# Attention mixed with the query and half of the output projections in one written TensorE order, with the residual parked in DRAM

## The chip, the cores and the metric

The kernel runs on one core of a Trainium2 chip. The metric is device time in microseconds (us), from the first to the last instruction of the program with what lies around it, as the median over runs.

## What is computed

One inference step of a two-layer decoder: layer 0 is a Mamba-2 mixer with a SwiGLU feed-forward, layer 1 is a sliding-window attention with a SwiGLU feed-forward. There are 1,104 rows of width 1,024: 1,024 prompt rows, 16 learned meta rows and 64 sampled rows (8 sequences of 8). The change lies between the two feed-forwards. Cut to that part, the reference is:

```python
kv_in = _rmsnorm(h, p['kv_norm_g'])                      # h: residual after layer 0
k_new = _rope_partial((kv_in @ p['w_k'])..., pos)        # 4 heads of 64
v_new = (kv_in @ p['w_v'])...
q = _rope_partial((_rmsnorm(h, g) @ p['w_q'][i])..., pos)  # 16 heads of 64
s = einsum(q, k) * HEAD_DIM**-0.5                        # masked to the last 128 keys
m = maximum(max(s), sink)
p = exp(s - m); p = p / (sum(p) + exp(sink - m))
h = h + einsum(p, v) @ p['w_o'][i]                       # output projection and residual
hn = _rmsnorm(h, p['ffn_norm_g'][layer])                 # and the second feed-forward on it
```

All arithmetic is fp32. Large products are done as three fp32r matmuls on a high and a low part of each operand (`mm3`, L71 to L73); attention uses plain fp32 matmuls.

## The kernel before, in words

**Order of work.** The program is written with a tile framework whose planner puts the instructions of each engine in order, by their place in the program and by simulated readiness; `tc.high_priority(n)` moves a block forward in that choice. `in_order` (L1001) chains a list of instructions of one engine, so that the planner keeps their written order. `mix(a, b, na, nb)` (L1020) advances two generators in the ratio na to nb while the program is written. All loads and stores that concern us are issued by one queue, SP's, in order.

**Stages around the change.** They follow each other on TensorE:

1. The layer-0 feed-forward ends with its down projection (`FeedForward.down`). Its input factors `bo` come from DRAM, six buffers. For each finished tile of 128 features, `Prepare.tile` squares it and splits it into operands for the next stage. The residual stays in SBUF as `K.h[0]` and `K.h[1]` (two column halves of 552: 40 sampled or meta columns and 512 prompt columns).
2. `qkv`: nine row blocks are multiplied by the key and value weights, then by the query weights in two halves of 512 columns (`rows_mm`, 24 matmuls of 512 columns for each block and half; `few_rows_mm` for the sampled rows). A finished block is scaled by ScalarE, rotated on GpSimd (`rope_rows`, six operations) and turned by four TensorE transposes into `A.QT` (`turn_queries`, L1963).
3. Attention: 16 units (`PromptUnit`: eight blocks of 128 queries, two head groups `a`), each with `scores(0)`, `scores(1)` (L2018, TensorE; L2024, masked maximum on VectorE), `softmax` (L2042, eight exponentials on ScalarE; L2045, two products on GpSimd), `turn` (12 transposes, L2060; copies L2063 and L2067) and `values` (L2078, L2082). Beside them `attend_sample` works through the eight sampled sequences in four steps each: keys turned (L2116), scores (L2127, L2128), a softmax on VectorE, ScalarE and GpSimd (L2140), its transposes (L2143, L2144), values (L2154, L2155). The planner is free to order all this on TensorE.
4. Output projection: attention's results are split into high and low parts (`split_copy`, L77 and L78), and for each column half e of 544 and each of eight feature tiles m, `output_tile` makes 48 matmuls of 272 columns, adds the product to the residual in place (L2179), squares the sum (L2180) and stores it to `F.saved` for the end of the second feed-forward. Its weights `wo` come through `F.units`, whose pool is opened after `qkv`.
5. `scale_early` and `early` prepare half 0 for the second feed-forward during the tiles of half 1 (`scaled`, L1272).

Of the kernel before, what the change touches and what calls it, by code (L numbers as in the profile page):

```python
# [51 lines left out]
ANA = 30  # L52
ANB = 33
# [1141 lines left out]
class FeedForward:  # L1195
# [50 lines left out]
    def save(self, e, m=None):  # L1246
# [7 lines left out]
        if self.layer == 0:  # L1254
            if e == 0:
                to(0, 0, h[0][:, :, 40:592])
                to(1, 0, h[0][:, :, 0:40])
            else:
                to(1, 40, h[1])
        elif m is not None:  # L1260
            to(e, 32, h[e][:, :, 40:552])
        elif e == 0:
            to(0, 0, h[0][:, :, 0:24])
            to(0, 24, h[1][:, :, 32:40])
        else:
            to(1, 0, h[1][:, :, 0:32])
# [7 lines left out]
    def few(self, dst, srcs, c):  # L1274
# [3 lines left out]
        o = 0  # L1278
        for s in srcs:
            w = s.shape[2]  # L1280
            rb = K.tot[:, c + o : c + o + w].unsqueeze(1).broadcast_to([128, KD, w])
            nc.vector.tensor_tensor(t[:, :, o : o + w], s, rb, ALU.mult)
            o += w
        nc.vector.tensor_tensor(dst, t, self.gain.unsqueeze(2).broadcast_to([128, KD, n]), ALU.mult)

    def scale_early(self, pool, psS):
# [12 lines left out]
        if self.layer:  # L1299
            self.few(h0[:, :, 8:40], [h0[:, :, 0:24], K.h[1][:, :, 32:40]], 0)  # L1300
# [41 lines left out]
    def late(self, k):  # L1342
# [3 lines left out]
        if self.layer and k == 0:  # L1346
            self.few(K.h[1][:, :, 8:40], [K.h[1][:, :, 0:32]], self.h)
# [418 lines left out]
class RowWeights:  # L1766
# [5 lines left out]
    def get(self, src, gain, stage, depth=KD):  # L1772
        nc, out = self.nc, []

        def load(k):
            if k < KD:
                t = stage(k)
                for a, b, s in src:
                    nc.sync.dma_start(t[:, a:b], s[128 * k : 128 * k + 128, :])
                out.append(t)  # L1780

        for k in range(depth):
            load(k)
        for k in range(KD):
            H = self.pool.tile([128, 512], F32R, name="rwH", tag="rwH", bufs=KD)
            L = self.pool.tile([128, 512], F32R, name="rwL", tag="rwL", bufs=KD)
            g = gain[:, k : k + 1]
            nc.scalar.activation(H[:], out[k], AF.Copy, scale=g)
            nc.vector.scalar_tensor_tensor(L[:], out[k], g, H[:].bitcast(F32), ALU.mult, ALU.subtract)
            out[k] = (H, L)  # L1790
            load(k + depth)
        return out


class Prepare:
# [5 lines left out]
    def __init__(self, tc, K, I):  # L1801
# [3 lines left out]
        self.U = [[None] * KD, [None] * KD]  # L1805

# [5 lines left out]
    def step(self, c, p):  # L1812
        I, K = self.I, self.K
        if c == 1 and p == 1:
            self.few = [self.wp.tile([128, KD, NX], F32R, name="ux" + x, tag="ux" + x) for x in "HL"]
            self.kv = self.weights.get([(0, 256, I["w_k"]), (256, 512, I["w_v"])], K.g_kv, lambda k: K.tot[:, 512 * (k % 2) : 512 * (k % 2) + 512], 2)
# [9 lines left out]
    def tile(self, e, m):  # L1826
# [20 lines left out]
        split_copy(nc, H, L, src)  # L1847
        self.seen[e] += 1
        if self.seen[e] == KD:
            self.small(e)  # L1850

# [25 lines left out]

def qkv(tc, K, A, ap, psS, I, O, pre):

    nc = tc.nc  # L1880
    with ExitStack() as st:
        en = lambda **kw: st.enter_context(tc.tile_pool(reuse_waits="tile", **kw))
        st.callback(pre.stack.close)
        fp = en(name="qf", bufs=1)
        psP = en(name="qps", bufs=4, space=PSUM)
        w = pre.kv
        cs = lambda i, n: A.rope[:n, 8 * i : 8 * i + 8]
        sn = lambda i, n: A.rope[:n, 72 + 8 * i : 80 + 8 * i]
        size = lambda i: 128 if i else NX
        start = lambda i: NX + 128 * (i - 1) if i else 0  # L1890
        r, r8 = {}, {}

        def scales(which, nm):
            blocks = [(128 * (i - 1) if i else 1024, size(i)) for i in which]
            t = row_scale(K, blocks, ap, psS.tile([128, 512], F32, name="ps", tag="s"))
            t8 = ap.tile([128, len(which)], F32, name=nm)
            nc.vector.tensor_scalar(t8[:], t[:], HD ** -0.5, None, ALU.mult)
            for x, i in enumerate(which):
                r[i], r8[i] = t[:, x : x + 1], t8[:, x : x + 1]

        def rows_mm(i, w):
            n = size(i)
            ps = psP.tile([128, 512], F32, name="rps", tag="rps")
            for k in range(KD):
                mm3(nc, ps[:n, :], *pre.operand(k, i), w[k][0][:], w[k][1][:], k == 0, k == KD - 1)
            return ps

        def few_rows_mm(w):

            ps = psP.tile([128, 512], F32, name="rps", tag="rps")  # L1910
            for k in range(KD // 2):
                for q in range(2):
                    f = KD // 2 * q + k
                    nc.tensor.matmul(
                        ps[64 * q : 64 * q + 64, :], hs[:, f, :], w(f), start=k == 0, stop=k == KD // 2 - 1, tile_position=(0, 64 * q)
                    )
            t = K.tot[:NS, 512:1024]
            nc.scalar.copy(t, ps[64:, :])
            nc.vector.tensor_tensor(t, t, ps[:64, :], ALU.add)
            return t  # L1920

        def put_kv(i, ps):
            n, o = size(i), start(i)
            kr = fp.tile([128, 256], F32, name="kr", tag="kr", bufs=2)
            nc.scalar.mul(kr[:n], ps[:n, 0:256], r[i][:n])
            nc.scalar.mul(A.V[:n, i, :], ps[:n, 256:512], r[i][:n])
            rope_rows(nc, fp, kr[:n], n, NKV, cs(i, n), sn(i, n), nc.gpsimd)
            pt = psS.tile([128, 512], F32, name="ps", tag="s")
            for a in range(2):
                nc.tensor.transpose(pt[:, 128 * a : 128 * a + n], kr[:n, 128 * a : 128 * a + 128], K.ident[:n, :n])  # L1930
            nc.scalar.copy(A.KT[:, :, o : o + n], pt[:, :256].rearrange("p (a c) -> p a c", a=2)[:, :, :n])
            if i == 0:
                pt = psS.tile([128, 512], F32, name="ps", tag="s")
                for kv in range(NKV):
                    nc.tensor.transpose(pt[:64, 64 * kv : 64 * kv + 64], kr[:NS, 64 * kv : 64 * kv + 64], K.ident[:NS, :NS])
                nc.scalar.copy(A.KS[:].rearrange("p a b -> p (a b)"), pt[:64, :256])
                for nm, t in (("k_s", kr[:NS]), ("v_s", A.V[:NS, 0, :])):
                    nc.sync.dma_start(O[nm][:, 120:128].rearrange("b l h d -> b l (h d)"), t)
            if i == 8:
# [441 lines left out]
```

## Time and profile before

| what | us |
|---|---|
| median of 3 runs | 2922.55 |
| lowest and highest run | 2916.72, 2922.65 |
| the profiled execution, its own time | 2921.38 |
| its span, first to last instruction | 2919.6 |
| TensorE busy by the page | 2804.8 |
| mean granted TensorE clock | 0.975 |

The profile is of one execution. "PE" is TensorE's matmuls, "PEld" its weight loads, "DVE" VectorE, "ACT" ScalarE, "POOL" GpSimd, "SP" the queue that issues transfers. Matmuls are pipelined: the time that one is said to last overlaps the next, so what it costs is read as the distance from its start to the next start. The granted clock is 1.00 at TensorE's full level (2.4 GHz) and 0.50 at the lower one (1.2 GHz).

### The profile page before, as it was taken

Reading aid. Unit: us, or ns where it says so; the run is one execution under the profiler, and the core shown is the slowest. Engines: PE = TensorE matmul, PEld = TensorE weight load, DVE = VectorE, ACT = ScalarE, POOL = GpSimd, SP = SyncE. Lnnn points to the kernel's source line nnn. Section 1 sums busy time; section 2 is a strip of 40 time slices with the busy share of each in tenths; the row PEclk is TensorE's granted clock in tenths of the full one; section 3 lists DMA queues with packets and bytes.
Section 4 is the critical chain, followed back from the end, with each engine's and each line's share of the span. In section 5 each row is a group of like instructions: output and inputs, shape, how many; then the busy total and the mean of one; then the engine's idle time right before and its main releaser. Section 6 shows DMA issues by size and latency. Waiting matters only on the chain.

```text
span 2919.6 us, 51250 instructions
## 1 busy us (share of the span) xinstructions
PE 2804.8 (96%) x19990; PEld 2577.6 (88%) x19990; DVE 2024.0 (69%) x3669; ACT 1218.7 (42%) x2592; POOL 494.9 (17%) x694
## 2 busy tenths in 40 slices
PE   7989999999999999999999999999998999999998
PEld 7878988887787799999999997765898999999998
DVE  6778676647574698777778771265469878777787
ACT  4666554346442344333332242256434433433224
POOL 1455444215122100000000002333120000000000
PEclk9999999999999999999999999969999999999999
DMA  6776866565454424444377640021232534437664
GB/s 205 238 232 190 282 200 208 188 234 202 169 181 149 159 97 168 135 146 149 135 282 281 221 146 33 22 65 36 68 89 78 178 129 157 150 136 293 239 226 154
DMA packets 321377, 485.44 MB, mean 166 GB/s; under 512 B 23967, under 2 KB 222047, under 8 KB 320081
## 3 DMA queue, kind: packets, MB, share of 16 engines
q1 hardware_dynamic: 321134, 482.15, 48.7%
q8 instruction: 158, 2.59, 0.4%
q14 instruction: 85, 0.70, 0.1%
HBM read 311.24 MB, written 170.84 MB: 165 GB/s over the span
## 4 chain that ended last, share of the span: by engine, by line
PE 68%; DVE 5%; ACT 2%; DMA 1%; issue 1%; POOL 0%; SPq 0%; ACTq 0%; DVEq 0%
PE wacc L1476 10%; PE wacc L1474 10%; PE wacc L1475 10%; PE dacc L1474 5%; PE dacc L1475 5%; PE dacc L1476 5%; PE acc L71 2%; PE acc L72 2%; PE acc L73 2%; PE rps L71 2%; PE rps L72 2%; PE rps L73 2%; PE po L2078 1%; PE ps L2018 1%; PE wacc L71 1%; PE wacc L72 1%
## 5 line engine op out<-in xcount | busy, mean ns | idle before, releaser
L1134 ACT CAST wo<-ws 128x512 fp32r<-128x512 f32 x428 | 263.7, 620 | 567.7 <-PE wacc L1475 222.9
L1474 PE MATMUL dacc<-bo,wo 128*128 128x276 f32 (+1 forms) x1232 | 359.3, 292 | 11.9 <-DMA bo<-f_B 7.8
L1475 PE MATMUL dacc<-bo,wo 128*128 128x276 f32 (+1 forms) x1232 | 356.7, 290 | 0.0
L1476 PE MATMUL dacc<-bo,wo 128*128 128x276 f32 (+1 forms) x1232 | 356.6, 290 | 0.0
L1135 DVE TENSOR_TENSOR wo<-ws,wo 128x512 fp32r<-128x512 f32 x428 | 300.3, 706 | 48.9 <-ACT wo L1134 30.1
L71 PE MATMUL acc<-uH,wH 128*128 128x296 f32 (+1 forms) x840 | 279.5, 333 | 1.9 <-DVE th L760 1.6
L72 PE MATMUL acc<-uL,wH 128*128 128x296 f32 (+1 forms) x840 | 278.0, 331 | 0.0
L73 PE MATMUL acc<-uH,wL 128*128 128x296 f32 (+1 forms) x840 | 276.4, 329 | 0.9 <-DVE wL L154 0.9
L1474 PEld LDWEIGHTS dacc<-bo,wo 128*128 128x128 f32 x1232 | 233.1, 189 | 13.8 <-issue 11.8
L1475 PEld LDWEIGHTS dacc<-bo,wo 128*128 128x128 f32 x1232 | 233.0, 189 | 0.0
L1476 PEld LDWEIGHTS dacc<-bo,wo 128*128 128x128 f32 x1232 | 232.9, 189 | 0.0
L71 PEld LDWEIGHTS acc<-uH,wH 128*128 128x128 f32 x840 | 161.4, 192 | 17.1 <-issue 5.0
L72 PEld LDWEIGHTS acc<-uL,wH 128*128 128x128 f32 x840 | 161.3, 192 | 12.0 <-issue 3.4
L73 PEld LDWEIGHTS acc<-uH,wL 128*128 128x128 f32 x840 | 160.9, 192 | 11.6 <-issue 2.0
L583 DVE SCALAR_TENSOR_TENSOR cc<-raw,convw,cc 128x616 f32<-128x616 f32 (+1 forms) x144 | 136.0, 947 | 40.6 <-ACT cc L581 38.6
L1622 DVE TENSOR_TENSOR hN<-hN,dacc 128x544 f32<-128x544 f32 (+1 forms) x164 | 116.4, 721 | 30.4 <-PE dacc L1476 25.5
L71 PE MATMUL acc<-yH,wH 128*128 128x296 f32 (+1 forms) x360 | 122.7, 341 | 8.8 <-ACT yH L77 5.2
L1058 POOL MEMSET rv<- 128x5 f32 (+1 forms) x6 | 0.6, 104 | 729.8 <-PE dacc L1476 723.5
L72 PE MATMUL acc<-yL,wH 128*128 128x296 f32 (+1 forms) x360 | 120.4, 335 | 0.0
L73 PE MATMUL acc<-yH,wL 128*128 128x296 f32 (+1 forms) x360 | 120.2, 335 | 0.0
L1474 PE MATMUL wacc<-N4H,wo 128*128 128x276 f32 (+1 forms) x352 | 102.0, 290 | 4.4 <-DVE hN L1487 2.4
L1474 PE MATMUL wacc<-T2H,wo 128*128 128x276 f32 (+1 forms) x352 | 101.8, 291 | 4.2 <-ACT T2H L77 4.2
(575 smaller groups left out, 8519.3 us busy)
## 6 DMA issues: line engine op xcount, KB each, us to landing
kept<-wH SPq DMA_DIRECT2D x56, 512.0 KB
kept<-wL SPq DMA_DIRECT2D x56, 512.0 KB
ws<-ffn_w_gate SPq DMA_DIRECT2D x44, 512.0 KB
ws<-ffn_w_up SPq DMA_DIRECT2D x44, 512.0 KB
ws<-ffn_w_down SPq DMA_DIRECT2D x44, 512.0 KB
ws<-ssm_w_in SPq DMA_DIRECT2D x40, 512.0 KB
wH<-kept SPq DMA_DIRECT2D x38, 512.0 KB
wL<-kept SPq DMA_DIRECT2D x38, 512.0 KB
```

The source lines that it names most:

```text
L71: nc.tensor.matmul(out, wH, xH, start=start, stop=False)
L72: nc.tensor.matmul(out, wH, xL, start=False, stop=False)
L73: nc.tensor.matmul(out, wL, xH, start=False, stop=stop)
L583: nc.vector.scalar_tensor_tensor(o, raw[:, k : k + n], w(k), o, ALU.mult, ALU.add)
L1134: nc.scalar.copy(H, src)
L1135: (low or nc.vector).tensor_tensor(L, src, H.bitcast(F32), ALU.subtract)
L1474: nc.tensor.matmul(out, wH, xH, start=start, stop=False, skip_group_check=True)
L1475: nc.tensor.matmul(out, wH, xL, start=False, stop=False, skip_group_check=True)
L1476: nc.tensor.matmul(out, wL, xH, start=False, stop=stop, skip_group_check=True)
L1622: add = lambda d, s: nc.vector.tensor_tensor(d, d, s, ALU.add)
L2018: nc.tensor.matmul(ps[e][:, 192 * s : 192 * s + kn], QT[es, hp, s], A.KT[es, a, self.k0[s] : self.k0[s] + kn], start=True, stop=True)
L2078: nc.tensor.matmul(out[s][e], A.V[:n, i + s, vs[e]], self.PT[e][:n, 256 * s : 256 * s + 256], start=True, stop=False)
```

## The change

The query projection, attention and half 0 of the output projection no longer follow each other; they are written interleaved, and TensorE keeps the written order from the first query block to the end of half 0.

- The units go through all blocks of head group 0 first, then of group 1. After three query blocks (`LEAD`), the other 13 are written between the steps of units 0 to 13 and of the sampled sequences, by `mix(att, qs, 96, 104)`: a query step is one of eight parts of a block (three matmuls), an attention step is one of `scores`, `turn` of one e, `values`, or a step of a sampled sequence.
- After the query weights are released, the weight pool opens, the results of twelve units and of the sampled rows are split with high priority, five attention steps go ahead (`AHEAD`), and the rest of attention is mixed with half 0 of the output projection (`output_early`), 4 to 5; a step there is two of the eight parts of a 272-column accumulation.
- PSUM: four rings of two banks (scores, turned, out, rows) take the place of three scores, three turned, two out and, in `qkv`, four rows.
- Attention's work tiles lie where the residual was (`A.space` on the tags h0 and h1). So the residual is stored to `F.saved` as the layer-0 feed-forward ends (`keep`, 16 tiles and three small pieces), `output_early` loads, adds to and stores one tile at a time, and both halves are loaded again before `output_tile`, which now does half 1 alone, with its TensorE instructions in written order. The stores of the finished half 0 take the place of those that were there before.

```diff
-def mix(a, b, na=1, nb=1):
+def joined(a, b, na=1, nb=1):      # as mix was, with a yield after each step
+def mix(*args):
+    for _ in joined(*args):
+        pass
...
+    def keep(self, e, fs):         # called by Prepare.tile and after its last tile
+        h, put = self.K.h[e], lambda i, a, b, o, n: self.nc.sync.dma_start(self.saved[i][:, fs, a:b], h[:, fs, o : o + n])
+        if fs.stop - fs.start == 1:
+            put(e, 32, 544, 40, 512)
...
+    w_q = lambda a: [(0, 512, I["w_q"][0][:, 512 * a : 512 * a + 512])]
+    raw = [[pre.weights.load(w_q(a), k, A.QT[:, k, a]) for k in range(KD)] for a in range(2)]
...
+    with tc.high_priority(PRIO):
+        w = [pre.weights.split(k, raw[0][k], K.g_attn) for k in range(KD)]
+    put_kv(*late.pop(0))
+    A.space = [K.cp.tile([128, n], F32, name="work", tag=f"h{e}") for e, n in enumerate((4736, 4416))]
...
+    def queries(w):
+        turned = [sampled_turned]
+        for a in range(2):
+            for i in range(1, 9):
+                for k, acc in enumerate(rows_mm(i, w)):
+                    if k == 5 and turned:
+                        turned.pop(0)()
+                    if k == KD - 1:
+                        dst = fp.tile([128, 512], F32, name="qr", tag="row", bufs=2)[:]
+                        put_q(i, acc, dst)
+                        turned.append(lambda i=i, a=a, dst=dst: turn_queries(i, a, dst))
+                    yield
...
+def output_early(nc, K, F, sqh, rows, oH, oL):
+    for m in range(KD):
+        u = F.units.get(1)
+        w = [u.factor(nm) for nm in ("lo", "hi")]
+        x = F.units.raw()[:, :544]
+        nc.sync.dma_start(x, F.saved[0][:, m])
+        F.units.load(2)
+        for c in range(2):
+            acc = rows()
+            cs = slice(272 * c, 272 * c + 272)
+            for k in range(KD):
+                wH, wL = (t[:, 128 * (k % 4) : 128 * (k % 4) + 128] for t in w[k // 4])
+                mm3(nc, acc[:, :272], wH, wL, oH[:, k, cs], oL[:, k, cs], k == 0, k == KD - 1)
+                if k == KD - 1:
+                    nc.vector.tensor_tensor(x[:, cs], x[:, cs], acc[:, :272], ALU.add)
+                    output_square(nc, K, F, sqh, x[:, cs], 0, m, 272 * c)
+                    if c:
+                        nc.sync.dma_start(F.saved[0][:, m], x)
+                if k % 2:
+                    yield
...
+                def prompt(first, last, done=lambda u: None):
+                    n = len(units)
+                    for x in range(first, last):
+                        if x < n:
+                            units[x].scores(0)
+                            yield
+                        if x >= 2:
+                            units[x - 2].turn(0)
+                            yield
+                        if x < n:
+                            units[x].scores(1)
+                            yield
+                        if 0 <= x - 1 < n:
+                            units[x - 1].softmax()
+                        if x >= 2:
+                            units[x - 2].turn(1)
+                            yield
+                            units[x - 2].values()
+                            done(units[x - 2])
+                            yield
+                forced = len(traced)
+                for _ in range(8 * LEAD):
+                    next(qs)
+                sample = attend_sample(tc, K, A, sp, ps, I, O, (4, 5, 6, 7, 0, 1, 2, 3))
+                att = joined(prompt(0, EARLY), sample, 5 * EARLY - 6, 32)
+                mix(att, qs, 5 * EARLY - 6 + 32, 8 * (16 - LEAD))
+            pre.stack.close()
             F.open_weights("left")
...
+            with tc.high_priority(PRIO):
+                for e, o, a, b in ((0, 0, 40, 64), (0, 24, 32, 40), (1, 0, 0, 32)):
+                    split_copy(nc, OH[e][:, :, o : o + b - a], OL[e][:, :, o : o + b - a], A.OS[:, :, a:b])
+                for u in units[: EARLY - 2]:
+                    split(u)
+            early = output_early(nc, K, F, sqh, ps.rows, OH[0], OL[0])
+            att = prompt(EARLY, len(units) + 2, split)
+            for _ in range(AHEAD):
+                next(att)
+            mix(att, early, 4, 5)
+            in_order(tc, traced[forced:], nc.tensor)
+            K.h = [K.cp.tile([128, KD, 552], F32, name=f"hN{e}", tag=f"h{e}") for e in range(2)]
+            for e in (1, 0):
+                for m in range(0, KD, 2):
+                    nc.sync.dma_start(K.h[e][:, m : m + 2, 8:552], F.saved[e][:, m : m + 2])
```

Here LEAD is 3, EARLY 14 and AHEAD 5. In the diff, comments behind a # are added for the reader.

## Rows read from the trace of the kernel before

**Rows 1.** The page, busy time over the whole span.
```profile
PE 2804.8 (96%) x19990; PEld 2577.6 (88%) x19990; DVE 2024.0 (69%) x3669; ACT 1218.7 (42%) x2592; POOL 494.9 (17%) x694
```

**Rows 2.** Windows: end of down projection, queries, attention, output half 0, half 1.
```profile
core 0: us, PE busy (x) PEld busy (x) DVE busy (x) ACT busy (x) POOL busy (x), PEclk, DMA share, GB/s
1562.00:1733.00 171.00, 170.65 (x1343) 170.43 (x1341) 142.59 (x225) 49.42 (x82) 0.14 (x2) 1.00 0.58 201
1787.70:1892.30 104.60, 104.60 (x477) 80.15 (x477) 18.50 (x27) 23.18 (x50) 33.30 (x113) 1.00 0.06 18
1892.30:2063.70 171.40, 158.34 (x1033) 101.18 (x1031) 97.80 (x466) 93.68 (x382) 56.82 (x62) 0.82 0.15 44
2063.70:2116.30 52.60, 49.01 (x385) 48.41 (x386) 26.76 (x49) 21.70 (x48) 7.79 (x5) 1.00 0.31 93
2116.30:2176.40 60.10, 56.20 (x431) 55.11 (x430) 39.58 (x79) 21.63 (x47) 17.91 (x8) 0.97 0.35 102
```

**Rows 3.** Windows: attention at the lower clock, and the rest of it.
```profile
1897.60:1945.40 47.80, 45.62 (x196) 27.97 (x198) 25.55 (x122) 22.59 (x94) 13.12 (x14) 0.50 0.30 83
1945.40:2063.70 118.30, 108.81 (x804) 70.39 (x800) 69.09 (x338) 69.74 (x285) 41.26 (x38) 0.94 0.10 30
```

**Rows 4.** Timeline of TensorE in attention: start, duration, line, operation, count, [idle before].
```profile
1957.24 0.92 PE L2018 MATMUL ps<-KT,QT 64*128 64x192 f32 x8
1958.09 0.66 PE L2060 MATMUL pq<-cmask_sb,P 128*128 128x128 f32 x4
1958.67 1.08 PE L2078 MATMUL po<-PT,V 128*64 128x256 f32 x4
1959.68 0.66 PE L2082 MATMUL po<-PM,V 64*64 64x256 f32 x8
1960.28 0.66 PE L2060 MATMUL pq<-cmask_sb,P 128*128 128x128 f32 x4
...
1965.33 1.56 PE L2018 MATMUL ps<-KT,QT 64*128 64x192 f32 x12
1966.83 0.30 PE L2154 MATMUL pq<-PTd,vst 128*64 128x32 f32 x2
1967.06 0.62 PE L2116 MATMUL pq<-cmask_sb,kst 128*64 128x128 f32 x4
1967.61 0.30 PE L2155 MATMUL pq<-PTd,V 64*64 64x32 f32 x2
...
1969.22 1.53 PE L2060 MATMUL pq<-cmask_sb,P 128*128 128x128 f32 x12
1970.68 0.44 PE L2127 MATMUL ps<-kT,q 64*32 64x128 f32 x8
...
1971.17 0.92 PE L2018 MATMUL ps<-KT,QT 64*128 64x192 f32 x8
...
1978.27 0.33 PE L2143 MATMUL pq<-cmask_sb,PD 128*128 128x128 f32 x1 [0.85 <-POOL PD L2140]
```

**Rows 5.** Timeline of TensorE in the query projection.
```profile
1803.36 0.39 PE L71 MATMUL rps<-rwH,u 128*128 128x512 f32 x1
...
1804.06 0.40 PE L71 MATMUL rps<-rwH,u 128*128 128x512 f32 x1
```

**Rows 6.** Groups by line in attention: ScalarE, VectorE, GpSimd (busy, mean ns, idle before).
```profile
L2042 ACT ACTIVATE P<-P,nm 128x192 f32<-128x192 f32 x112 | 49.5, 445 | 7.3 <-DVE es L2035 7.3
L2063 ACT COPY PT<-pq 128x512 f32<-128x512 f32 x28 | 15.9, 580 | 15.1 <-PE pq L2060 15.1
L2045 POOL TENSOR_TENSOR P<-P,sm 128x768 f32<-128x768 f32 x28 | 41.0, 1466 | 53.0 <-DVE sm L2044 39.7 <-DVE es L2035 7.7 <-DVE sm L2043 3.0
```

**Rows 7.** Groups by line in output half 0, VectorE.
```profile
L78 DVE TENSOR_TENSOR OL<-O,OH 128x544 fp32r<-128x544 f32 x16 | 10.5, 720 | 0.9 <-ACT OH L77 0.6
```

**Rows 8.** The chain that ended last, around half 1 of the output projection.
```profile
2139.67 3.60 DVE hN L1272 x6
```

More of the change, by code (lines that the diff above doesn't have):

```diff
@@ L51 @@
 FIRST = 3
-ANA = 30
-ANB = 33
+LEAD = 3
+EARLY = 14
+AHEAD = 5
+PLACES = {"scores": ("S", 2), "turned": ("T", 2), "out": ("O", 2), "rows": ("P", 2)}
 HALVES = (
@@ L1770, in __init__, with load, split @@
         self.nc, self.pool = nc, pool
[L1772 to L1792, printed above, removed]
+    def load(self, src, k, t):
+        for a, b, s in src:
+            self.nc.sync.dma_start(t[:, a:b], s[128 * k : 128 * k + 128, :])
+        return t
+    def split(self, k, t, gain):
+        nc = self.nc
+        H = self.pool.tile([128, 512], F32R, name="rwH", tag="rwH", bufs=KD)
+        L = self.pool.tile([128, 512], F32R, name="rwL", tag="rwL", bufs=KD)
+        g = gain[:, k : k + 1]
+        nc.scalar.activation(H[:], t, AF.Copy, scale=g)
+        nc.vector.scalar_tensor_tensor(L[:], t, g, H[:].bitcast(F32), ALU.mult, ALU.subtract)
+        return H, L
 class Prepare:
@@ L1875, in close, with qkv @@
         pass
[L1878 removed]
+def qkv(tc, K, A, ap, fp, ps, O, I, pre):
     nc = tc.nc
[L1881 to L1939, printed above, removed]
[L1940 to L1987 removed]
@@ new lines, in rows_mm, with few_rows_mm @@
+    def rows_mm(i, w):
+        n = size(i)
+        acc = ps.rows()
+        for k in range(KD):
+            mm3(nc, acc[:n, :], *pre.operand(k, i), w[k][0][:], w[k][1][:], k == 0, k == KD - 1)
+            yield acc
+    def few_rows_mm(w):
+        acc = ps.rows()
+        for k in range(KD // 2):
+            for q in range(2):
+                f = KD // 2 * q + k
+                nc.tensor.matmul(
+                    acc[64 * q : 64 * q + 64, :], hs[:, f, :], w[f], start=k == 0, stop=k == KD // 2 - 1, tile_position=(0, 64 * q)
+                )
+        t = K.tot[:NS, 512:1024]
+        nc.scalar.copy(t, acc[64:, :])
+        nc.vector.tensor_tensor(t, t, acc[:64, :], ALU.add)
+        return t
@@ new lines, in qkv, with __init__, ring, get @@
+    return queries(w)
+class Space:
+    def __init__(self, work):
+        self.work, self.used, self.rings = work, [0, 0], {}
+    def ring(self, name, where, size, count):
+        o = self.used[where]
+        self.used[where] += size * count
+        assert self.used[where] <= self.work[where].shape[1]
+        self.rings[name] = [[self.work[where][:, o + size * i : o + size * i + size] for i in range(count)], 0]
+    def get(self, name, rows=128):
+        r = self.rings[name]
+        r[1] += 1
+        return r[0][(r[1] - 1) % len(r[0])][:rows]
@@ L2236, in attention @@
             F.units.queue += ups
[L2237 removed]
+            F.units.load(2)
             so = ExitStack()
             op = so.enter_context(tp(name="ao", bufs=1))
[L2240 to L2242 removed]
@@ new lines, in attention @@
+        steps, tiles = iter(()), []
+        for m in range(KD):
+            at = len(traced)
+            with tc.high_priority(60 if m else 0):
+                output_tile(nc, K, F, sqh, OH[1], OL[1], m)
+            tiles += traced[at:]
+            for _ in range(3):
+                next(steps, END)
+            if m == 0:
+                steps = chain(F.scale_early(F.wp, F.psS), F.early())
+        in_order(tc, tiles, nc.tensor)
+        for _ in steps:
+            pass
+        with tc.high_priority(PRIO):
+            F.late_scale(F.psS)
```

415 lines of the change are left out of this document (203 added, 212 removed).

## The prediction

> **What bounds the kernel now.** I read the page first. It puts TensorE at 96% of the span [rows 1], and a reader could stop there: at most 4% would be left. So the second view is the windows by stage. In the query projection TensorE is busy throughout at the full clock, with its weight loads at 80.15 of 104.6 us. In attention the two rows part: matmuls are busy 158.34 of 171.4 us, weight loads only 101.18, and the mean clock is 0.82 [rows 2]. The third view cuts attention at its clock. For 47.8 us the clock is at its lower level, and in the other 118.3 us it has dips (0.94) [rows 3]. No other engine is full: VectorE 97.80, ScalarE 93.68, GpSimd 56.82 of 171.4 us [rows 2]. So attention has neither a full TensorE nor a full neighbour: it waits in chains between engines.
>
> How much TensorE attention really needs I take from the timeline at the full clock, by distances between starts, because durations overlap. Eight score matmuls take 0.85 us (1957.24 to 1958.09) and twelve 1.50 (1965.33 to 1966.83), so 0.1175 each; sixteen transposes 0.58 + 1.46, so 0.1275 each; four L2078 take 1.01, eight L2082 0.60 [rows 4]. A unit has 16, 12, 8 and 8 of them: 1.88 + 1.53 + 2.02 + 0.60 = 6.03 us, and 16 units 96.5. A sampled sequence has four key transposes (0.55), scores (1970.68 to 1971.17, 0.49), two transposes (0.26) and 16 small value matmuls at 0.23 a pair, as the last seven pairs show (1967.61 to 1969.22), 1.84: 3.14 us, eight of them 25.1. The last turned queries and the sampled queries (8 and 16 transposes, the latter smaller, at up to 0.1275) add some 2 us. The stage needs 123.6 us and takes 171.4: **47.8 us are surplus**. Half of the slow stretch, 23.9 us, is the clock; the other half is waiting that busy time hides.
>
> The Trainium skill (Perfetto Trace Analysis, Identifying the Most-Contended Engine) says that matmul busy time is a poor measure of TensorE's headroom and names weight-load busy time as a good one. The trace agrees: 92% by matmuls, 59% by weight loads, 72% by my distances. By the busy row the surplus would be 171.4 - 158.3 = 13.1 us, and the sum below would end at +7, a slower kernel.
>
> **The change part by part.**
>
> *Interleaving, gain.* The query parts fill the chains' waits. A part is three matmuls of 512 columns, 0.70 us [rows 5]. If TensorE never waited, the mixed stages would cost what their matmuls cost and the 47.8 us would go. I take all of it, and then charge the waits that the written order makes. That counts on the clock staying full: between attention steps now stand dense full-array matmuls, of the kind that held 1.00 for 104.6 us, turning transposes included [rows 2].
>
> *Waits in the first mix.* In written order one late operand holds everything behind it. Between two attention steps stands one query part; a sampled step comes after every second unit step.
> - `turn(1)` to `values`: the copy L2063 takes 0.58 us [rows 6]; in front of its reader stand 0.70 and the first 0.25 us of `values`, 0.95. By durations it is covered, and behind one exponential (0.445) it is late by 0.1; the hand-offs between engines are in no duration, and I allow 0.4 for them. Bounds 0 and 0.5; I take the middle, 0.25 x 16 = 4 us.
> - Sampled scores to transposes: as run, 1971.17 to 1978.27, 7.1 us, and TensorE then waited 0.85 for GpSimd [rows 4]. The cover is two unit steps (6.03/5 each) and three parts, 4.5 us. Bounds: 0 and 2.6 x 8 = 21. The 7.1 us hold queueing behind exponentials that a planner with a fixed TensorE order can put later, so I take 0.6 x 8 = 5.
> - `scores(0)` to `scores(1)`, and turned tiles, with two banks each: about 2 us of other work stands between, and the maxima are short. Taken as 0, at most 0.3 x 16 = 5.
> - The start: the sampled queries are turned in the first block, so TensorE waits for two scalings and six GpSimd rotations after `few_rows_mm`, behind the split of eight weight tiles. Bounds 0 and 5; 2 taken, near one GpSimd product (1.47 [rows 6]).
>
> GpSimd's queue now mixes rotations with the unit products (two of 1.47 us a unit); its 33.3 + 56.8 us in the two stages' 104.6 + 123.6 = 228 leave it more than half idle. ScalarE and VectorE sum to 117 and 116 us of the same 228 [rows 2]. None becomes the bound.
>
> *The seam between the mixes.* The weight pool opens as the last query block ends. Twelve splits with high priority (0.72 us each for 544 columns [rows 7], so 0.68 for 512: 8 us with the sampled pieces about 9) go ahead on VectorE of the maxima of units 14 and 15 and of the first `wo`. Five attention steps, 6 us, stand before the first output matmul, but two of these wait for VectorE too. Below, if splits start early, 0; above 9. I take 5.
>
> *Output half 0.* The same matmuls; the stage was 52.6 us, 4.4 of it in gaps for `wo` that I leave in. The residual's add is the same size in two pieces.
>
> *Half 1.* Its splits no longer lie beside half 0; its add and square are one operation each. Taken as 0, at best -3.
>
> *The residual.* Stores of 16 x 256 KB are now issued at the end of the down projection, on SP's queue between the loads of `bo`, which TensorE needs just in time. DMA is 0.58 busy there at 201 GB/s [rows 2]; 3 MB more over the last 70 us is 45 GB/s. TensorE has 0.35 us idle in that window, so the loads have been in time. VectorE's 142.59 of 171 us is the danger: a store that waits for it holds the loads behind. Bounds 0 and 5; 1 taken. The reload is 4.4 MB, at the 201 GB/s of that window 22 us. Half 1 can be loaded once attention's last value is copied, some 41 us before half 0 ends (by the 4:5 mix 50 of its 64 steps stand alone, and all took 52.6). Half 0 is first needed by `scaled`, at 2139.67, 23 us after half 0 ended [rows 2, 8]. Both are covered; uncovered, the second would cost its 11.
>
> *Clock dips* like those in the second part of attention: 3 us, bounds 0 and 7 (6% of 118.3 [rows 3]).
>
> **Sum:** -47.8 + 4 + 5 + 2 + 5 + 1 + 3 = -27.8 us. From the profiled execution's 2921.4 (span 2919.6 and 1.8 around it; the median is 1.2 above) that is 2893.6; I say **2894**.
>
> **Rivals.**
>
> *The order waits more than the gaps were worth (slower).* In the mixed stages stand 112 unit and sampled steps up to the end. If the mean wait before a step exceeds 47.8/112 = 0.43 us, nothing is left. For it: the 7.1 us chain and the copies, whose upper bounds alone give 21 + 8, with 5 for the banks, 5 at the start, 9 at the seam, 7 for the clock, 55 in all: 2929. Against it: no engine would be much above half busy, and each unit's softmax has a whole round, some 14 us, for 3.6 us of exponentials. Chance 12%.
>
> *The clock falls all the same.* The matmuls of attention stay what they were, with some 200 transposes, and at the start of attention the clock fell with TensorE busy 45.62 of 47.8 us [rows 3]. If the mix is held at the lower level for as long, the 23.9 us come back: 2894 + 24 = 2918, a gain within reach of noise. Against it: the query stage's 1.00. The Trainium skill (TensorE: Matmul & The Clock Gate, Part 4: PE-mode transpose) says that transposes do not count as busy for the clock as matmuls do, which speaks for this rival; the query stage, with four transposes in each block, shows it harmless there. Chance 8%.
>
> *Nearly all waits are covered.* The planner fits the other engines to the fixed order, and only the small terms stay: -47.8 + 8, 2881 and below to 2870 with half 1 shorter. For it: no engine is full. Chance 20%.
>
> *Transfers.* Stores delay `bo`, reloads delay half 0: 4 + 11 on top, 2909. Against: 0.31 and 0.35 DMA share in the output stages [rows 2]. Chance 6%.
>
> **How the numbers follow.** The forecast has 54%; with the two that only change its size, faster has 80%. A measurement of this kernel tells about 0.2%, 6 us: its runs spread over 5.9. The clock's 2918 is faster by 0.15%, so of its 8% half counts as faster and half as the same, and 2 more as the same from the slow rival's near edge: 0.84, 0.06, 0.10. The range leaves out the slow rival's far part below one in ten and the best case beyond 2872: 2872 to 2920; the forecast's own is 2884 to 2904.
>
> **What would show it.** After: the stretch from the first sampled query product to the end of half 0 (1787.7 to 2116.3 before, 328.6 us [rows 2]) is about 301. In it the clock row is near 1.00 and TensorE's weight loads are busy well above 59%. TensorE's waits are many and short, led by L2140 and the copies. At the seam there is one gap of some 5 us. No wait for `bo` at the end of the down projection, none for the reloaded residual. Wrong would be: a second long stretch at 0.50, a mean wait of 0.4 us before attention's steps, or half 1 that starts late.

## The result, and the profile after

The changed kernel takes 2893.81 us (median of 4 runs, 2886.74 to 2895.70) beside 2922.49 us before (2916.72 to 2922.65): ratio 0.9902, interval [0.9881, 0.9923]. Forecast were 2894 and a range of 2872 to 2920. The profiled execution took 2894.77 us, its span is 2893.0.

The page of the changed kernel, busy time over the whole span (answers to [rows 1]):

```profile
PE 2779.4 (96%) x19990; PEld 2554.9 (88%) x19990; DVE 2028.3 (70%) x3655; ACT 1221.7 (42%) x2580; POOL 488.4 (17%) x692
```

TensorE's busy share is 96% as before, with the same number of matmuls. It shows nothing of the change, so the stages have to be read. Windows of the changed kernel (columns as in [rows 2]): end of the down projection; first mix, from the first sampled-query product to the last query part; the seam, up to the first output matmul; second mix, to the end of half 0; half 1; then first mix to half 0 in one, and to half 1.

```profile
core 0: us, PE busy (x) PEld busy (x) DVE busy (x) ACT busy (x) POOL busy (x), PEclk, DMA share, GB/s
1566.00:1738.00 172.00, 172.00 (x1355) 172.00 (x1354) 143.80 (x227) 49.38 (x82) 0.00 (x0) 1.00 0.66 226
1792.20:2011.20 219.00, 208.39 (x1361) 140.61 (x1360) 104.09 (x433) 102.41 (x377) 78.71 (x151) 1.00 0.10 28
2011.20:2033.10 21.90, 13.93 (x57) 8.10 (x56) 16.28 (x42) 13.69 (x33) 3.67 (x8) 0.55 0.09 26
2033.10:2093.50 60.40, 60.17 (x479) 55.80 (x478) 28.06 (x67) 27.78 (x72) 15.63 (x16) 0.99 0.64 182
2093.50:2149.90 56.40, 51.62 (x407) 51.17 (x407) 40.66 (x71) 18.51 (x34) 10.68 (x7) 0.97 0.48 148
1792.20:2093.50 301.30, 282.49 (x1894) 204.51 (x1894) 148.43 (x542) 143.88 (x481) 98.02 (x175) 0.97 0.21 59
1792.20:2149.90 357.70, 334.11 (x2299) 255.68 (x2299) 189.09 (x613) 162.38 (x514) 108.69 (x182) 0.97 0.25 73
```

From the first sampled-query product to the end of half 0 it took 328.6 us before [rows 2] and takes 301.3. The first mix, nearly three quarters of it, runs at a granted clock of 1.00 throughout; the second is at 0.99. Between them stand 21.9 us at 0.55: the one bad place that is left. The sum of the two profiled executions: start of the stretch 1787.7 to 1792.2, +4.5; the stretch to half 0, -27.3; half 1, 60.1 to 56.4, -3.7; the rest 743.2 to 743.1, -0.1. Together -26.6, the difference of the spans. The +4.5 is no work of the change: TensorE, VectorE and ScalarE run the same instructions up to there, and over the profiles of this kernel and its variants that start lay between 1780.5 and 1792.2, and the variant with twice the stores starts at 1783.5.

TensorE's timeline in the first mix, changed kernel (start, duration, line, operation, [idle before]), shows the order as written:

```profile
1901.07 0.27 PE L2105 MATMUL pT<-cmask_sb,work 128*128 128x128 f32 x1
1901.10 0.48 PE L73 MATMUL pP<-rwH,u 128*128 128x512 f32 x1
1901.42 0.39 PE L74 MATMUL pP<-rwL,u 128*128 128x512 f32 x1
1901.64 0.40 PE L75 MATMUL pP<-rwH,u 128*128 128x512 f32 x1
1901.88 0.60 PE L1998 MATMUL pT<-cmask_sb,qr 128*128 128x128 f32 x4
1902.41 0.65 PE L2123 MATMUL pO<-work,V 128*64 128x256 f32 x2
1904.66 1.08 PE L2123 MATMUL pO<-work,V 128*64 128x256 f32 x6 [1.60 <-ACT work L2107]
1905.67 0.66 PE L2127 MATMUL pO<-work,V 64*64 64x256 f32 x8
```

A transpose step (L2105), a query part (L73 to L75), the turn of a query block (L1998), then `values` (L2123, L2127), which here waited 1.60 us for ScalarE's copy of the turned probabilities. TensorE's waits in all, changed kernel (what waited <- what ended it: us in total, times, longest). In the first mix:

```profile
PE pO L2123 <- ACT work L2107: 4.9, 4, 1.6
PE pT L2178 <- POOL work L2175: 3.1, 4, 1.6
PE pO L2123 <- ACT work L2109: 2.3, 2, 1.3
PE pS L2066 <- DVE work L2072: 0.2, 1, 0.2
```

At the seam:

```profile
PE pT L1998 <- POOL qr L1773: 3.7, 1, 3.7
PE pO L2123 <- DVE work L2112: 3.1, 1, 3.1
PE pS L2066 <- DVE work L2072: 1.2, 2, 0.9
```

In the second mix and half 1:

```profile
PE ps L1071 <- POOL tot L2204: 4.8, 1, 4.8
PE pO L2123 <- DVE work L2112: 0.2, 1, 0.2
```

10.5 us in 219 of the first mix, 8.0 in the 21.9 of the seam, and one of 4.8 at the end of half 1, for the row sums that `late_scale` needs. None in the down projection or for the reloaded residual. Three pieces of the chain that ended last show where the 4.8 us come from (changed kernel: start, duration, what):

```profile
2137.81 4.77 DMA ws<-ffn_w_up
2145.83 0.64 DVE hN L2243
2149.03 0.27 PE ps L1071 x2
```

On VectorE, work on a weight of the second feed-forward, which had to be loaded first, stands ahead of an add of half 1, and the row sums need that add. The copies and products that attention's steps wait for, as groups by line in the first mix (changed kernel, columns as in [rows 6]):

```profile
L2107 ACT COPY work<-pT 128x512 f32<-128x512 f32 x20 | 11.6, 582 | 26.4 <-PE pT L2105 26.4
L2092 POOL TENSOR_TENSOR work<-work 128x768 f32<-128x768 f32 x23 | 33.8, 1468 | 67.8 <-DVE work L2091 66.8 <-DVE work L2173 0.6 <-ACT qr L1956 0.4
```

Both durations are those of [rows 6]: the neighbours did not become slower in the mix. So a wait for a copy is mostly not the copy's own 0.58 us. In the case above the last transpose of L2105 ended at 1901.34, and ScalarE came to the copy only at 1904.05, after exponentials that stood ahead of it in its order. The seam, changed kernel, TensorE first and then ScalarE's and VectorE's splits and VectorE's copy:

```profile
2010.99 0.39 PE L75 MATMUL pP<-rwH,sum 128*128 128x512 f32 x1
2015.07 1.11 PE L1998 MATMUL pT<-cmask_sb,qr 128*128 128x128 f32 x4 [3.69 <-POOL qr L1773]
2016.11 1.65 PE L2066 MATMUL pS<-KT,QT 64*128 64x192 f32 x8
...
2024.51 1.86 PE L2123 MATMUL pO<-work,V 128*64 128x256 f32 x4
2029.43 1.12 PE L2123 MATMUL pO<-work,V 128*64 128x256 f32 x4 [3.07 <-DVE work L2112]
...
2013.94 6.34 ACT L79 CAST OH<-QT 128x512 fp32r<-128x512 f32 x12
2021.32 4.90 DVE L80 TENSOR_TENSOR OL<-QT,OH 128x512 fp32r<-128x512 f32 x8
2028.70 0.68 DVE L2112 COPY work<-pO 128x512 f32<-128x512 f32 x1
```

The last query block must be scaled, rotated on GpSimd and turned before unit 15 can be scored, and here no query part is left to put between: TensorE stands 3.69 us, and the clock is at its lower level from 2013.4 to 2033.9. Eight score matmuls start over 1.58 us (2016.11 to the next operation at 2017.69) where they took 0.85 in [rows 4]. Then the copy L2112 comes late. Its products had ended at 2026.37, but VectorE still had maxima and a subtraction in front of it, held up by its eight subtractions from 2021.32 on.

### The profile page after: what moved, and what is told of

Read it like the earlier page. It is cut to its first block, busy times and chain, and to the rows that moved or that the text cites. A ratio compares the mean times of both kernels' runs of the same rounds, so it can differ in the third digit from the quotient of the medians.

```text
span 2893.0 us, 51252 instructions
## 1 busy us (share of the span) xinstructions
PE 2779.4 (96%) x19990; PEld 2554.9 (88%) x19990; DVE 2028.3 (70%) x3655; ACT 1221.7 (42%) x2580; POOL 488.4 (17%) x692
## 4 chain that ended last, share of the span: by engine, by line
PE 83%; DVE 7%; DMA 4%; ACT 3%; issue 2%; POOL 1%; SPq 0%; ACTq 0%; DVEq 0%; POOLq 0%
PE wacc L1486 10%; PE wacc L1484 10%; PE wacc L1485 10%; PE acc L73 6%; PE acc L74 6%; PE acc L75 6%; PE dacc L1484 5%; PE dacc L1485 5%; PE dacc L1486 5%; PE pP L73 2%; PE pP L74 2%; PE pP L75 2%; PE ps L670 1%; PE ps L667 1%; DVE cc L585 1%
## 5 line engine op out<-in xcount | busy, mean ns | idle before, releaser
L73 PE MATMUL acc<-uH,wH 128*128 128x296 f32 (+1 forms) x840 | 279.9, 333 | 0.9 <-DVE th L762 0.6
L75 PE MATMUL acc<-uH,wL 128*128 128x296 f32 (+1 forms) x840 | 276.8, 329 | 0.9 <-DVE wL L156 0.9
L1484 PEld LDWEIGHTS dacc<-bo,wo 128*128 128x128 f32 x1232 | 233.8, 190 | 12.7 <-issue 10.3
L73 PEld LDWEIGHTS acc<-uH,wH 128*128 128x128 f32 x840 | 161.9, 193 | 16.4 <-issue 4.1
L74 PEld LDWEIGHTS acc<-uL,wH 128*128 128x128 f32 x840 | 161.6, 192 | 12.7 <-issue 4.2
L75 PEld LDWEIGHTS acc<-uH,wL 128*128 128x128 f32 x840 | 161.4, 192 | 11.6 <-issue 2.0
L73 PE MATMUL acc<-yH,wH 128*128 128x296 f32 (+1 forms) x360 | 123.1, 343 | 10.9 <-ACT yH L79 5.1
L75 PE MATMUL acc<-yH,wL 128*128 128x296 f32 (+1 forms) x360 | 120.4, 336 | 0.0
L1143 ACT CAST wo<-sum 128x512 fp32r<-128x512 f32 x66 | 41.0, 621 | 154.3 <-PE wacc L1485 110.9
```

Source lines behind the costliest of these rows:

```text
L73: nc.tensor.matmul(out, wH, xH, start=start, stop=False)
L74: nc.tensor.matmul(out, wH, xL, start=False, stop=False)
L75: nc.tensor.matmul(out, wL, xH, start=False, stop=stop)
L1143: nc.scalar.copy(H, src)
L1484: nc.tensor.matmul(out, wH, xH, start=start, stop=False, skip_group_check=True)
```

## The experiments

Every comparison is with the kernel before on the same chip; "stretch" is the time from the first sampled-query product to the end of half 1 in the run's profile (388.7 before, 357.7 in the changed kernel).

**The changed kernel once more**, nothing edited.

> The changed kernel once more, unedited, to stand beside the next three on one chip: 0.990 of the kernel before, 2888 to 2896 us; in its profile the stretch from the first sampled query product to the end of output half 1 takes 358 us, give or take 4, with a half-clock stretch at the seam.

2894.96 us (2886.46 to 2896.81), ratio 0.9916 [0.9898, 0.9934]. Windows of this run:

```profile
1788.20:2150.50 362.30, 338.07 (x2298) 257.64 (x2298) 189.25 (x613) 162.40 (x514) 108.56 (x182) 0.96 0.24 72
```

The stretch is just outside what was expected (358, give or take 4). Two profiles of one kernel differ by 4.6 us in the stretch, and 3.2 of these lie in the first mix:

```profile
1788.20:2010.40 222.20, 211.59 (x1361) 142.26 (x1360) 104.17 (x433) 102.39 (x377) 78.55 (x151) 0.98 0.10 28
```

Its waits are the same to a tenth (4.9, 3.1, 2.3 and 0.2 us), but here the clock was at its lower level for some 7 us (1962 to 1969). So a clock of 1.00 throughout is the first profile's, not every execution's. The kernels below that keep both the first mix and its written order have stretches of 359.7 to 365.2: differences of this size say nothing.

**The mix and the written order, apart.** One kernel runs the queries first, then attention, in a written order; one does so with the planner's order for TensorE; one keeps the mix and gives the planner the order.

```diff
-LEAD = 3
+LEAD = 16
...
-                mix(att, qs, 5 * EARLY - 6 + 32, 8 * (16 - LEAD))
+                for _ in chain(qs, att):
+                    pass
```

> All 16 query blocks stand ahead of attention, in written order; the second mix with output half 0 stays. Theory (the query parts fill the waits of attention's chains and hold the clock): the first 12 units and the sampled rows, some 101 us of TensorE work, run alone again; before, 123.6 us of such work took 171.4, a factor of 1.39, so about 39 us come back and more if the written order waits longer without cover: 2930 to 2945 us, with a long stretch at the lower clock. Rival (the gain came from what stays here: unit order, PSUM rings, written order, the second mix): within 6 us of 2894.

The second has that and, as the third alone, this:

```diff
-            in_order(tc, traced[forced:], nc.tensor)
```

> As the run with all queries first, but TensorE's order is the planner's, as it was before the change. Theory: without query parts to fill with, attention costs what it cost before: 2915 to 2935 us, with the lower clock in it, and less than the written order without cover. Rival (the gain came from unit order, rings and the second mix): within 6 us of 2894.

> The change with the written TensorE order taken away: the mix is written, the planner orders TensorE. Theory (the gain lies in what is there to fill with, not in fixing it): within 8 us of 2894, either side. Rival (the planner undoes the mix, so the fixed order is what brings the gain): over 2905, with attention's waits back.

Queries first, written order: 2937.47 us (2932.13 to 2939.00), ratio 1.0066 [1.0042, 1.0090]. Queries first, planner's order: 2919.62 (2900.20 to 2928.11), 1.0000 [0.9978, 1.0021]. Mix, planner's order: 2900.74 (2888.42 to 2905.87), 0.9939 [0.9916, 0.9961]. Windows of the stretch in the first:

```profile
1782.40:2188.00 405.60, 362.72 (x2299) 280.25 (x2299) 194.40 (x613) 163.58 (x514) 109.60 (x182) 0.89 0.22 64
```

in the second:

```profile
1786.30:2182.50 396.20, 378.21 (x2298) 287.19 (x2298) 187.73 (x613) 162.81 (x514) 108.52 (x182) 0.89 0.22 66
```

and in the third:

```profile
1783.70:2154.10 370.40, 357.31 (x2299) 271.84 (x2299) 188.39 (x613) 161.30 (x514) 108.33 (x182) 0.95 0.24 71
```

Stretch of the profile, and median of the runs, in us:

| | planner's order | written order |
|---|---|---|
| queries first | 396.2; 2919.62 | 405.6; 2937.47 |
| mixed | 370.4; 2900.74 | 357.7 and 362.3; 2893.81 and 2894.96 |

Mixing is shown under either order: it gives 25.8 us of stretch under the planner and 47.9 (or 43.3 by the second profile) in written order, and the ratios' intervals lie apart. Unit order, PSUM rings, the second mix and the parked residual are in the queries-first kernels too, and with the planner's order they bring nothing (1.0000). That the written order costs time without the mix is shown as well: 17.9 us by the medians, and 9.4 by two profiles of which one is that kernel's slowest run (2928.11) and the other its kernel's fastest (2932.13). That it gives something with the mix is not: the stretch is 8.1 to 12.7 us shorter, but the medians, from different chips, differ by 5.8 to 6.9 us and the ratios' intervals overlap, as the theory of the third kernel had it (within 8 us of 2894). The longest waits of TensorE, up to the output projection, in queries first with written order:

```profile
PE pT L2178 <- POOL work L2175: 10.5, 4, 3.8
PE pO L2123 <- ACT work L2107: 8.4, 6, 3.3
PE pS L2066 <- DVE work L2072: 8.2, 7, 2.3
PE pS L2066 <- DVE work L2169: 3.5, 4, 1.2
```

Mostly the same readers wait as in the changed kernel. These four rows are 30.6 us, with five smaller ones 39.3, where the changed kernel waits 10.5 + 8.0 = 18.5 up to its first output product. The clock goes with it, 0.89 without the mix and 0.95 to 0.97 with it. The waits differ by 20.8 us; no run changes the clock alone, so how much of the rest of the 47.9 is clock isn't separated.

**The second mix taken out**: the rest of attention, then half 0.

```diff
-            for _ in range(AHEAD):
-                next(att)
-            mix(att, early, 4, 5)
+            mix(chain(att, early), iter(()), 1, 1)
```

> The first mix stays; the last units run to their end alone, in written order, before output half 0 begins. Theory (output products fill the waits of the last units too): the rounds of units 14 to 17 steps, 13 us of TensorE work in the second mix, which ran without a wait there, take a factor of 1.4 or more alone, and the seam's splits have nothing beside them: 5 to 12 us more, 2899 to 2906. Rival (the seam costs the same whatever stands behind it): within 4 us of the changed kernel.

2895.56 us (2892.87 to 2899.43), ratio 0.9927 [0.9910, 0.9943]. Windows of the rest of attention and of half 0:

```profile
2009.90:2049.70 39.80, 27.82 (x149) 15.07 (x148) 25.78 (x76) 25.54 (x71) 9.80 (x12) 0.74 0.10 28
2049.70:2098.60 48.90, 48.90 (x393) 48.70 (x389) 18.85 (x34) 17.19 (x33) 9.56 (x12) 1.00 0.73 232
```

Together 88.7 us, where seam and second mix take 82.3. The expected loss isn't there by the runs: the ratio's interval overlaps the changed kernel's. By the profile the second mix gives 6.4 us at this place, little more than two profiles differ by, and the whole stretch, 363.0, is within 0.7 us of the second profile above. The first mix carries nearly the whole gain.

**The residual's transfers doubled**: every tile's store and every reload is issued twice.

```diff
-        self.F.keep(e, slice(m, m + 1))
+        for _ in range(2):
+            self.F.keep(e, slice(m, m + 1))
...
-                for m in range(0, KD, 2):
+                for m in [x for m in range(0, KD, 2) for x in (m, m)]:
```

> Every store of the residual at the end of the layer-0 feed-forward is issued twice, and every reload before half 1 too: 4.2 MB written and 4.5 MB read on top. Theory (this traffic is hidden beside TensorE with room to spare): within 4 us of the changed kernel, TensorE still without a wait for a transfer in the down projection. Rival (transfers are just in time there and near full at the end of half 0): 5 to 15 us more, with waits for bo or hN.

2890.72 us (2889.89 to 2892.21), ratio 0.9910 [0.9894, 0.9925]. Window of the end of the down projection in this run:

```profile
1559.00:1730.00 171.00, 171.00 (x1345) 170.92 (x1345) 142.79 (x225) 49.46 (x82) 0.31 (x4) 1.00 0.69 241
```

TensorE is busy throughout with twice the stores on the queue, and nothing waits for the reload. The transfers are hidden.

**Five ways at what is left.** First, the last turn of a query block five steps later, so that its rotation is done.

```diff
+TAIL = 5
...
+        for _ in range(TAIL):
+            yield
...
-                mix(att, qs, 5 * EARLY - 6 + 32, 8 * (16 - LEAD))
+                mix(att, qs, 5 * EARLY - 6 + 32, 8 * (16 - LEAD) + TAIL)
```

> Five empty query steps are put ahead of the last turned block, and the mix is 96 to 109, so that TensorE no longer meets the GpSimd rotation of the last block (3.7 us of waiting at the seam, after which the clock fell for some 20 us). Theory A (that wait starts the seam's loss): 4 us and part of the half-clock loss go, 2883 to 2890. Theory B (the seam is bound by VectorE's splits, the wait only stands ahead of them): within 3 us of 2894.

2893.23 us (2886.99 to 2903.54), ratio 0.9920 [0.9898, 0.9942]. The wait of 3.7 us is gone. The longest waits of TensorE in this run, over the whole stretch (L2126 and L2110 are L2123 and L2107 there):

```profile
PE pO L2126 <- ACT work L2110: 13.4, 5, 5.8
```

Its window of the seam:

```profile
2001.90:2023.10 21.20, 15.25 (x105) 9.14 (x104) 18.54 (x56) 19.51 (x63) 4.78 (x8) 0.84 0.05 14
```

At the seam one copy now keeps TensorE 5.8 us, with ScalarE, which has the splits' casts, busy 19.51 of 21.2 us; the other 7.6 us lie in the first mix. The clock rose from 0.55 to 0.84, and the seam is as long, but it holds more: 105 matmuls in place of 57, some 14 us of work at the prediction's prices in place of 7.7. This work came out of the first mix, which took 221.4 us for 6 us less of it, with the clock at 0.97. First mix and seam together took 242.6 us, where the changed kernel's two profiles have 240.9 and 244.1: what the seam gained the first mix lost.

Second, the splits without priority; third, both edits together.

```diff
-            with tc.high_priority(PRIO):
+            with tc.high_priority(0):
```

> The splits of twelve units at the seam lose their high priority, so the maxima of units 14 and 15 and the copies go ahead on VectorE and ScalarE. Theory (the seam's 22 us for 7.5 us of TensorE work come from the splits standing ahead of attention's last rounds): the seam shortens by 3 to 6 us, 2888 to 2891. Rival (the splits are needed by the first output product anyhow, so they only change places): within 3 us of the changed kernel.

> Two edits together: the last block is turned five steps later, and the twelve splits have no priority. Alone, the first moved the wait to copies behind the splits, the second left the 3.7 us behind the rotation. Theory (each hides the other's gain): the seam, 22 us for 7.5 us of TensorE work, shortens by 6 to 10 us, and its half-clock stretch with it: 2884 to 2889. Rival (the clock sets the seam): within 3 us of the changed kernel.

2889.72 us (2887.41 to 2891.45), 0.9903 [0.9887, 0.9920], and 2892.72 (2884.89 to 2902.64), 0.9920 [0.9899, 0.9941]: no clear difference from the changed kernel in either. The seam is 21.5 us in both, with 57 matmuls in the first and 105 in the second. So the first one's time lies in its forecast without the shorter seam that was to bring it.

Fourth, half of the twelve subtractions on GpSimd.

```diff
-            def split(u):
+            def split(u, shared=False):
...
+                if shared and (u.i + u.a) % 2:
+                    nc.scalar.copy(OH[e][:, fs, o : o + 128], u.O)
+                    nc.gpsimd.tensor_tensor(OL[e][:, fs, o : o + 128], u.O, OH[e][:, fs, o : o + 128].bitcast(F32), ALU.subtract)
+                    return
...
-                    split(u)
+                    split(u, True)
```

> Six of the twelve subtractions at the seam go to GpSimd, which is idle there (about 1.0 us each by its rate, 6 us beside VectorE's 4 in place of 8). Theory (VectorE's queue of splits makes the seam): 3 to 4 us less, 2890. Rival (ScalarE's twelve casts, 6.3 us in one piece, or the clock bind it as well): within 2 us.

2895.70 us (2886.75 to 2897.75), ratio 0.9917 [0.9898, 0.9936]; the seam is 22.1 us. Timeline of GpSimd and VectorE in this run:

```profile
2010.18 8.16 POOL L2359 TENSOR_TENSOR OL<-QT,OH 128x512 fp32r<-128x512 f32 x6
2013.15 4.07 DVE L80 TENSOR_TENSOR OL<-OS,OH 128x192 fp32r<-128x192 f32 x3
2017.14 1.75 DVE L80 TENSOR_TENSOR OL<-QT,OH 128x512 fp32r<-128x512 f32 x1
2019.83 0.68 DVE L80 TENSOR_TENSOR OL<-QT,OH 128x512 fp32r<-128x512 f32 x1
```

While GpSimd subtracts (to 2018.34), one subtraction of 128x512 on VectorE takes 1.75 us, and 0.68 after it. Three of 128x192 take 4.07 there, 1.36 each, as long as one on GpSimd; in the changed kernel the three took 0.82. GpSimd's own six took 1.36 each, where 1.0 was expected. What GpSimd took over, VectorE lost again: the maxima came late, and TensorE waited 5.6 us for them at the seam in place of 1.2.

Fifth, against the 4.8 us wait at the end of half 1: half 0's row sums and column scale begun one output tile later, and, since that missed the place, its row sums written behind the second output tile of half 1 and its column scale behind the third, on top of the third kernel above.

```diff
-            if m == 0:
+            if m == 1:
                 steps = chain(F.scale_early(F.wp, F.psS), F.early())
```

> The scaling of half 0 is begun one output tile later, so that its row sums no longer stand on TensorE before the last squares are added (one wait of 4.8 us behind GpSimd at the start of half 1). Theory (that wait is on the path): 3 to 5 us less, 2889 to 2891. Rival (half 0 is then ready later for the second feed-forward, which waits by as much): within 2 us of the changed kernel.

The second, without the lines of the third kernel that it stands on:

```diff
             r = row_scale(K, blocks, pool, ps)
+        if self.layer:
+            yield
...
+            if m == 1:
+                steps = chain(F.scale_early(F.wp, F.psS), F.early())
+            if m in (1, 2):
+                next(steps)
...
-            for _ in range(3):
+            for _ in range(3 if m > 2 else 0):
                 next(steps, END)
-            if m == 0:
-                steps = chain(F.scale_early(F.wp, F.psS), F.early())
```

> As the run with both edits at the seam, and the row sums of half 0 are written behind the second output tile of half 1, its column scale behind the third, both in TensorE's written order. Theory: the 4.8 us wait behind GpSimd's squares goes, and half 0 is still scaled before the second feed-forward needs it: 3 to 5 us less than the run with two edits, 2880 to 2886. Rival (the second feed-forward then waits for the scaled half): no less, or more.

2887.50 us (2886.17 to 2890.97), 0.9898 [0.9882, 0.9915], and 2889.67 (2887.20 to 2892.32), 0.9906 [0.9891, 0.9920]. Both rest on a misreading: the waiting row at 2149.03 has 128x1 products for the row sums of half 1, not of half 0, so neither edit reaches it; in the first it is still there, 4.9 us. In the second a new wait of 6.3 us for VectorE's `tot` came at half 0. Nothing follows of the wait at the end of half 1, whose chain, shown above, begins with the transfer of a weight, and no kernel here is clearly faster than the changed one.

## Why the prediction was right, point by point

The total came out as forecast; some of its terms did not, and they cancel. At the prediction's prices the work up to half 0 is 104.6 (queries) + 123.6 (attention) + 48.2 (half 0 without its gaps) = 276.4 us. It took 301.3, so 24.9 us are above it; forecast were 23.4: 19 in waits and dips, and the 4.4 of gaps left in half 0. Where they lie is told by the matmul counts of each window: the seam's 24 scores, 16 transposes, eight L2123, eight L2127 and the end of a query part are 2.8 + 2.0 + 2.0 + 0.6 + 0.3 = 7.7 us; the second mix has 13.4 us of attention and 48.2 of half 0, 61.6; so 207.1 is left for the first.

| | at the prices | taken | above | forecast |
|---|---|---|---|---|
| first mix | 207.1 | 219.0 | 11.9 | 11 (4 + 5 + 0 + 2), and most of 3 for dips |
| seam | 7.7 | 21.9 | 14.2 | 5 |
| second mix | 61.6 | 60.4 | -1.2 | 4.4 |

- *The surplus of 47.8 us in attention is taken back by the mix*: right. It is shown by the queries-first kernels, whose stretch is 47.9 us longer in written order, and 38.5 in the planner's. That the first figure is so near the surplus is chance, since there only twelve of the 16 units run alone and the written order adds waits of its own. Costing TensorE by the distance of starts was what made the sum come out; by busy rows it would have ended at +7.
- *Waits of the first mix*: right in sum, and in who waits; the split was off and cancels. Copies 4.9 + 2.3 = 7.2 us (4 forecast), sampled scores to transposes 3.1 (5), banks 0.2 (0), no wait at the start (2). The copies were priced at 0.25 us for each of 16 units, for hand-offs between engines. They cost six waits of 1.2 us on average instead, in the case above behind ScalarE's exponentials, and a hand-off is short: the copy above ends at 1904.61 and its reader starts at 1904.66. The mean wait before a step stayed far below the slow rival's 0.43 us: 10.5 us over 96 steps, 0.11 each.
- *The seam*: the step that was mis-sized, 14.2 us against 5. The forecast named the late maxima behind the splits. The runs show two things more. The last block's scale, rotation and turn have nothing left to hide them (3.7 us of the 8.0 idle). And at half clock the 7.7 us of work took 13.9, 6.2 more, a term that the sum had only as 3 us of scattered dips. What limits it stays open. Without the splits' priority, or with half of the subtractions elsewhere, it takes 21.5 and 22.1 us. Turned later, it does 14 us of work in 21.2 to 21.5 us, with the clock at 0.80 to 0.84, but no kernel with that edit is clearly faster.
- *Half 0*: its 4.4 us of gaps [rows 2] were to stay and went; TensorE is busy 60.17 of 60.4 us in the second mix.
- *Half 1*: 3.7 us shorter, a little beyond the best end of the forecast (3), but most of that is bookkeeping. In the kernel before, 23 feed-forward matmuls were put inside half 1; at 0.126 us each (the distance of starts at full clock) that is 2.9 us of work that now stands behind it. Going by the unchanged 743.1 us of the rest, it costs nothing there. A reason is likely, not shown: from 23.6 us after half 1 on VectorE is busy nearly throughout, as this window of the changed kernel has it.

```profile
2173.50:2193.50 20.00, 15.65 (x106) 14.28 (x105) 19.56 (x31) 13.62 (x24) 0.00 (x0) 0.94 0.00 1
```

- *The residual*: hidden, 0 for 1, shown by the doubled transfers. The DMA share at the end of the down projection rose from 0.58 to 0.66, and TensorE had no wait.
- *The clock*: 1.00 through the first mix in one profile and 0.98 in the other, so the rival that held the mix at the lower level as long as before (47.8 us) fell. What is left of it are the 20.5 us at the seam. The Trainium skill (TensorE: Matmul & The Clock Gate, Part 4: PE-mode transpose) says that transposes do not count as busy for the clock as matmuls do, which spoke for that rival. With some 200 full transposes between dense products the changed kernel's two profiles show no loss and one of some 3 us; without dense products between them, in the queries-first kernels, the clock of the stretch is 0.89.
- *Weight loads busy well above 59%*: 68% in the stretch that was named (204.51 of 301.3), but a poor sign. The 59% was attention alone; the same stretch had 70% before (80.15 + 101.18 + 48.41 of 328.6 [rows 2]), so the share fell as the kernel became faster.

## What to carry to other kernels

When a stage of short dependent chains stands beside a stage of long independent products, cost both by the distances between starts at the full clock; what the chain stage takes above that is what mixing can return, less the waits that the mixed order makes. Do not fix the order of the engine that bounds without such a mix: here that cost 17.9 us by the medians. With the mix, a gain from the fixed order was not clear of noise. Look for the place where the filler runs out, and price it with the clock it will have.

## What the runs showed of the hardware

A subtraction of 128x512 (fp32 to fp32r) took 0.68 us on VectorE alone and 1.75 beside the same operation on GpSimd, which took 1.36 each (no run has it alone). Three of 128x192 took 0.82 us alone and 4.07 beside it. The Trainium skill (SBUF — State Buffer, Who interferes with whom) says that a VectorE instruction with two SBUF inputs contends with a GpSimd instruction that reads SBUF; the run agrees, and moving part of such work to GpSimd gained nothing. In the changed kernel's first profile the granted clock held 1.00 for 219 us in which TensorE waited eleven times for up to 1.6 us, and went to 0.50 during a wait of 3.7 us at the seam. In its second profile, with the same order and the same waits, it was also at 0.50 for some 7 us within the first mix.
